# Applying the per-chunk triangular inverses ahead of the recurrence in a one-core RWKV-7 and attention step

## The chip, the core and the metric

The kernel runs on one core of one Trainium2 chip, in float32 throughout. The metric is the device time of one execution in microseconds (us), the median of several runs. The engines are named as in the profile: PE is the matrix engine (TensorE), PEld its weight loads, DVE the vector engine, ACT the scalar engine, POOL GpSimd, and SP the engine whose queue issues most of the DMAs. A name such as L503 is line 503 of the kernel before; where a line of the changed kernel is meant, the text says so.

## What is computed

One inference step of one layer: a combined projection of 1,024 prompt tokens and 32 sample tokens (8 sequences of 4) by `w_in` (1,024 x 9,344), then two branches side by side, RWKV-7 time mixing and dilated window attention, then a gated merge, an output projection and a layer norm. The change lies in the RWKV-7 branch. Its recurrence in the reference, for 8 heads of 64 with the state S[value, key]:

```python
def step(S, inp):
    r_t, w_t, k_t, v_t, kk_t, a_t = inp
    sa = jnp.einsum('bhvk,bhk->bhv', S, -kk_t)
    S = (S * w_t[:, :, None, :] + sa[..., None] * (kk_t * a_t)[:, :, None, :]
         + v_t[..., None] * k_t[:, :, None, :])
    return S, jnp.einsum('bhvk,bhk->bhv', S, r_t)
```

## The kernel before

**Products.** The projection is cut into columns of 128 (`project_steps`, L174). Each has its weights split into a high and a low part (L162 on ACT, L163 on DVE) and takes 72 matmuls of 128 x 352 (`mm3`, L172, tile `pj`); the scheduler below hands them out in pieces of four. These "products" are most of PE's work. Twelve columns (key, receptance, value for four pairs of heads) feed the recurrence, one (columns 1536 to 1663) its decay and its a; 24 others are "fill" (gates, written to DRAM through the tile `zt`) and can run at any time. The very first column is the gate column 1664, done while the input is still being transposed; then comes column 1536, then the stage with streams.

**The recurrence.** A unit is a pair of heads and half of the sequence (512 tokens), so there are 8 units; a unit has 8 chunks of 64 tokens, each with its two heads. For a chunk the token-by-token recurrence becomes matrices: with kappa the normalised key times the running decay, A the 64 x 64 lower triangle of a chunk, and T its inverse. `unit` (L309) prepares a unit: norm of the keys (L313, `rsqrt`), the two small lora products (L294), decay (L330 to L337: `lam`, `E`, `Ei`), kappa and rho in the tile KR (L346, L347), the tile BK (L355, L356), the masked triangles AT (16 matmuls in two halves, L370, masked on DVE in L377), the bonus (L389), the transposed values (L397) and keys (L407), and R0 (L416). `inverse` (L429) inverts the 32 x 32 diagonal blocks on DVE (L441, L444) with the blocks carried through DRAM; `scan` (L454) joins the blocks to the 64 x 64 inverses (L467, L477) and then walks through the 8 chunks one after another:

1. pr = (rho, kappa) times state (L496); R = pr + R0 on DVE (L498).
2. u = inverse times R: two 64 x 64 x 64 matmuls, one a head (L503); ACT negates and copies it into W (L504).
3. new state from W and BT (L508), scaled and added on DVE (L511).

So a chunk has three matmul steps on PE with a DVE or ACT instruction between each two. At the unit's end L519 computes the outputs of all chunks, and `norm` normalises them (L548 transposes).

**The order on PE** is written by `run_streams`, a planner inside the kernel. Four generators (`scans`, `norms`, `inverses`, `units`) yield pairs of numbers: what the step costs PE and how long to wait before the next step. At each turn the first generator whose waiting time is over goes on; if none can, four product matmuls are put in the queue, counted as 0.59 us. The other engines' queues are filled by a scheduler outside of the kernel's text. In `unit`, L331 waits until the scan of the unit two back is done, since the tiles E and KR have two buffers; everything of the preparation from E on stands behind that line.

## Time and profile before

| | us |
|---|---|
| median of 3 runs (lowest, highest) | 1380.13 (1377.95, 1381.62) |
| the profiled execution's own time | 1381.54 |
| its span, first to last instruction | 1379.8 |
| PE busy in the span | 1344.1 |
| first matmul of the first unit (L313) | at 76.78 |
| last matmul of the recurrence's streams (L548) | at 616.88 |

The profiled execution is 1.41 us above the median. Starts of instructions on PE are exact, ends of matmuls are modelled: a matmul of 128 x 352 is shown with 0.3 us though one starts every 0.16 us. So what PE's time goes into is read here from the distances between starts, not from the busy column: a row "x4" is four matmuls in a run, and the next row's start less its own is what it took PE.

### The profile page before, as it was taken

What the parts mean: (1) busy time and instruction counts of PE and PEld (TensorE: products, weight loads), DVE (VectorE), ACT (ScalarE), POOL (GpSimd) and SP (SyncE); (2) the same over time, 40 slices, a digit from 0 to 9 for tenths busy, and PEclk for the clock granted to TensorE, in tenths of its full rate; (3) what the DMA queues carried; (4) which work ended last, traced back from release to release, by engine and by line L of the source; (5) the groups of instructions that cost most, each with busy time, mean ns of one, the idle gap of its engine ahead of it and who ended that gap; (6) DMA issues with size and microseconds to landing.
All of it is one profiled execution on the core that took longest, in us unless ns stands there. A gap on an engine that the chain in (4) does not pass through costs nothing.

```text
span 1379.8 us, 25342 instructions
## 1 busy us (share of the span) xinstructions
PE 1344.1 (97%) x9809; PEld 1245.0 (90%) x9809; DVE 804.0 (58%) x2203; ACT 467.2 (34%) x1089; POOL 67.2 (5%) x82
## 2 busy tenths in 40 slices
PE   7999999999999999999999999999999999899997
PEld 7998998898988889999999999999999998799786
DVE  4358767677867757441555275437542845665565
ACT  4333434444344444431332333233323234132211
POOL 0000000000000000000100000000000000015100
PEclk9999999999999999999999999999999999999999
DMA  6112222412322242336645355635554556795221
GB/s 216 55 47 73 58 82 72 110 37 75 88 59 75 74 110 79 91 94 123 136 106 132 84 141 115 131 93 140 114 123 115 133 122 153 230 287 170 82 103 68
DMA packets 340270, 151.62 MB, mean 110 GB/s; under 512 B 188928, under 2 KB 329622, under 8 KB 339894
## 3 DMA queue, kind: packets, MB, share of 16 engines
q1 hardware_dynamic: 241270, 129.68, 34.6%
q10 hardware_dynamic: 98880, 20.32, 7.4%
q8 instruction: 77, 1.26, 0.4%
q14 instruction: 43, 0.35, 0.1%
HBM read 110.68 MB, written 38.97 MB: 108 GB/s over the span
## 4 chain that ended last, share of the span: by engine, by line
PE 74%; DVE 14%; DMA 7%; issue 2%; ACT 2%; SPq 1%; DVEq 0%; ACTq 0%
PE pj L172 52%; PE pj L1378 7%; DVE tm L441 2%; DVE X L444 2%; PE o L932 2%; DMA cb<-cd 2%; PE s L895 2%; DMA wraw<-in_w_in_dram 1%; DVE wlo L163 1%; DVE o L1178 1%; PE t L915 1%; PE sc L503 1%; PE s L1014 1%; PE g L370 1%; DVE AT L377 1%
## 5 line engine op out<-in xcount | busy, mean ns | idle before, releaser
L172 PE MATMUL pj<-xhi,whi 128*128 128x352 f32 x1848 | 398.7, 337 | 5.0 <-ACT xhi L1245 3.0
L172 PE MATMUL pj<-xlo,whi 128*128 128x352 f32 x1848 | 382.8, 328 | 0.0
L172 PE MATMUL pj<-xhi,wlo 128*128 128x352 f32 x1848 | 381.9, 328 | 0.4 <-DVE wlo L163 0.4
L172 PEld LDWEIGHTS pj<-xhi,whi 128*128 128x128 f32 x1848 | 302.9, 189 | 21.7 <-issue 10.5
L172 PEld LDWEIGHTS pj<-xhi,wlo 128*128 128x128 f32 x1848 | 307.6, 189 | 3.6 <-issue 1.2
L172 PEld LDWEIGHTS pj<-xlo,whi 128*128 128x128 f32 x1848 | 307.9, 189 | 2.5 <-issue 0.4
L163 DVE TENSOR_TENSOR wlo<-wraw,whi 128x512 fp32r<-128x512 f32 x162 | 113.4, 701 | 84.0 <-ACT whi L162 83.3
L162 ACT ACTIVATE whi<-wraw 128x512 fp32r<-128x512 f32 x162 | 100.6, 625 | 146.6 <-PE pj L172 89.0
L905 ACT ACTIVATE Sm<-Sm,nm 128x128 f32<-128x128 f32 (+1 forms) x96 | 42.4, 442 | 102.7 <-DVE nm L902 102.7
L511 DVE SCALAR_TENSOR_TENSOR st<-sc,E,SD 64x64 f32<-64x64 f32 x128 | 36.2, 283 | 47.7 <-PE sc L508 46.2
L441 DVE TENSOR_TENSOR tm<-Y,X 128x60 f32<-128x60 f32 (+24 forms) x248 | 52.6, 212 | 6.3
L444 DVE TENSOR_TENSOR X<-X,tm 128x60 f32<-128x60 f32 (+24 forms) x248 | 52.0, 210 | 6.4
L1378 PE MATMUL pj<-wl,mh 128*128 128x512 f32 (+1 forms) x136 | 52.0, 382 | 0.0
L897 DVE CUSTOM_DVE_ANT_0 Sm<-s,cst 128x128 f32<-128x128 f32 (+1 forms) x96 | 29.2, 346 | 39.0 <-PE s L895 38.3
L494 ACT ACTIVATE SD<-st,E 128x128 f32<-128x128 f32 x64 | 25.6, 400 | 58.5 <-DVE st L511 58.5
L758 POOL TENSOR_TENSOR kvp<-vv,kv 128x512 f32<-128x512 f32 x16 | 19.7, 1233 | 514.3 <-DVE Ss L766 387.0
L932 PE MATMUL o<-PT,Vt 128*128 128x128 f32 x280 | 38.7, 276 | 0.8 <-ACT PT L919 0.8
L895 PE MATMUL s<-k,q 128*128 128x128 f32 (+1 forms) x192 | 37.8, 326 | 1.7 <-DVE ml L897 1.6
L820 ACT ACTIVATE k<-pj 128x352 f32<-128x352 f32 (+1 forms) x36 | 16.2, 454 | 67.5 <-PE pj L172 60.9
L932 PEld LDWEIGHTS o<-PT,Vt 128*128 128x128 f32 x280 | 36.4, 191 | 1.5 <-ACT PT L919 1.1
L503 PEld LDWEIGHTS sc<-R,AT 64*64 64x64 f32 x256 | 19.7, 134 | 18.4 <-DVE R L498 7.9
L299 ACT ACTIVATE zt<-pj,der 128x352 f32<-128x352 f32 x48 | 26.4, 551 | 27.9 <-PE pj L172 26.7
(314 smaller groups left out, 1719.1 us busy)
## 6 DMA issues: line engine op xcount, KB each, us to landing
wraw<-in_w_in_dram SPq DMA_DIRECT2D x146, 256.0 KB
gd<-zt SPq DMA_DIRECT2D x48, 176.0 KB
gt<-gd SPq DMA_DIRECT2D x48, 176.0 KB
vs<-bt ACTq DMA_DIRECT2D x48, 128.0 KB
kc<-in_cache_kv_g_dram SPq DMA_DIRECT2D x48, 128.0 KB
Vt<-vs ACTq DMA_DIRECT2D x12, 512.0 KB
cb<-cd SPq DMA_DIRECT2D x12, 512.0 KB
zd<-zt SPq DMA_DIRECT2D x24, 176.0 KB
```

The source lines that it names most:

```text
L162: S.activation(hi[:], raw[:], AF.Copy)
L163: V.tensor_tensor(lo[:], raw[:], hi.bitcast(F32)[:], ALU.subtract)
L172: T.matmul(out, w[wi][:, n % 4, :], x[:, n % 4, :], start=first and n == 0, stop=last and n == 11)
L441: V.tensor_tensor(tm, Y[:, r : r + 1, r + 1 : 32].to_broadcast([P, m, n]), X[:, 0:m, r : r + 1].to_broadcast([P, m, n]), ALU.mult)
L444: V.tensor_tensor(X[:, 0:m, r + 1 : 32], X[:, 0:m, r + 1 : 32], tm, ALU.subtract)
L503: T.matmul(pu[u, 64 * e : 64 * e + 64], AT[u, e, c, u], R[u, 64 * e : 64 * e + 64], start=True, stop=True)
L511: V.scalar_tensor_tensor(S1[d, d], pS[d, d], E[d, c, 64:65], SD[d, d], ALU.mult, ALU.add)
L895: T.matmul(r, qT[:, i * P : (i + 1) * P], kT[:, keys[i][0] * P : keys[i][0] * P + n], start=True, stop=True)
L897: V.tensor_tensor_reduce(out=Sm[:, i, 0:n], in0=r, in1=m3 if g == 2 else m12[:, 256 - n : 256], scale=1.0, scalar=NEG, op0=ALU.add, op1=AL ...
L905: S.activation(Sm[:, i, 0:n], Sm[:, i, 0:n], AF.Exp, scale=SCALE, bias=nm[:, x : x + 1], accum_out=ml[:, g, 1, i : i + 1])
L932: T.matmul(po[:, (i % 4) * P : (i % 4 + 1) * P], st["Vt"][:, kb_, :], PT[:, n * P : (n + 1) * P], start=m == 0, stop=m == len(keys[i]) - 1,)
L1378: T.matmul(pb[:], a[:, k], wk, start=x == 0, stop=x == len(prods) - 1)
```

## The change

Four things are changed together.

**Inverses applied beforehand.** `scan` transposes kappa once for a unit (4 transposes, and two copies into kT), applies all 16 inverses to kappa in one batch of 16 matmuls (64 x 64 x 64), writes the result over kappa in KR, then applies all 16 inverses to R0 in a second batch of 16. In a chunk, step 2 above is gone: the sum pr + R0 on DVE is written to W directly. A chunk has two matmul steps.

**Preparation before the wait.** In `unit` the wait for the scan two back moves behind Ei, the normalised key, bt, f2, k2 and BK; behind it stay E, KR and rk.

**The planner.** D_HOP goes from 0.99 to 1.25, D_PM from 0.53 to 0.9, D_AT from 7.0 to 3.5, D_WU is gone, D_U0 is new. And `units` and `norms` may only go on while `small`, the planner's sum of small work not yet followed by products, is below 1.0.

**The first projection** is column 1536 (decay and a); column 1664 joins the fill.

The diff, cut to its core:

```diff
     lam = t_()
     V.tensor_tensor_scan(lam[:], rmask, sg[:], 0.0, ALU.mult, ALU.add)
-    while done["scan"] < 2 * j + hf - 1:
-        yield None
-    E = mk(rp, [P, 8, 65], "E", 2)
...
     V.tensor_tensor(BK[:, :, 0:4:3, :], c2p(k2), c2p(Ei), ALU.mult)
+    yield (0.45, 0.0)
+    while done["scan"] < 2 * j + hf - 1:
+        yield None
+    E = mk(rp, [P, 8, 65], "E", 2)
...
+    KR = mk(rp, [P, 4, 4, 64], "KR", 2)
+    V.tensor_tensor(KR[:, :, 1:3, :], c2p(kkn), Ev[:, :, :, 0:64], ALU.mult)
+    V.tensor_tensor(KR[:, :, 0:4:3, :], c2p(Mr[:, sl]), Ev[:, :, :, 1:65], ALU.mult)
     rk = t_()
...
+    pk = ps("sc")
+    for c2 in range(4):
+        T.transpose(pk[:, c2 * P : (c2 + 1) * P], KR[:, c2, 1:3, :], ident)
+    kT = mk(rp, [P, 512], "sz", 2).rearrange("p (a b) -> p a b", a=4)
+    for p in range(2):
...
+        S.activation(kT[u], pk[v, :].rearrange("p (a b) -> p a b", a=4), AF.Copy)
+    yield (0.45, 0.5)
...
+    pk = [ps("sc") for p in range(2)]
+    for c2, p, e in chunks:
+        u = slice(64 * (1 - p), 64 * (1 - p) + 64)
+        T.matmul(
+            pk[p][64 * e : 64 * e + 64, 64 * c2 : 64 * c2 + 64],
+            kT[u, c2, 64 * e : 64 * e + 64], AT[u, e, 2 * c2 + p, u], start=True, stop=True,
+        )
+    for p in range(2):
+        S.activation(KR[:, :, 1 + p, :], pk[p][:, 0:256].rearrange("p (a b) -> p a b", a=4), AF.Copy, scale=-1.0)
+    yield (1.0, D_PM)
+    pu = ps("sc")
+    for c2, p, e in chunks:
+        u = slice(64 * (1 - p), 64 * (1 - p) + 64)
+        T.matmul(
+            pu[u, c2 * P + 64 * e : c2 * P + 64 * e + 64],
+            AT[u, e, 2 * c2 + p, u], R0[u, c2, 64 * e : 64 * e + 64], start=True, stop=True,
+        )
+    S.activation(R0[:], pu.rearrange("p (a b) -> p a b", a=4), AF.Copy, scale=-1.0)
+    yield (1.0, D_U0)
...
-        R = mk(rp, [P, P], "R", 1)
-        V.tensor_tensor(R[u], pr[u, 0:P], R0[u, c2, :], ALU.add)
+        V.tensor_tensor(W[u, c, :], pr[u, 0:P], R0[u, c2, :], ALU.add)
         S.activation(Ot[v, c2, :], pr[v, 0:P], AF.Copy)
         yield (0.2, D_HOP)
-        pu = ps("sc")
-        for e in range(2):
-            T.matmul(pu[u, 64 * e : 64 * e + 64], AT[u, e, c, u], R[u, 64 * e : 64 * e + 64], start=True, stop=True)
-        S.activation(W[u, c, :], pu[u, 0:P], AF.Copy, scale=-1.0)
-        yield 0.4, D_WU
...
-                if x[0] <= now:
+                if x[0] <= now and (small < SMALL or x in own or not prods):
```

The order of PE's instructions in the middle of a unit's scan before, from one chunk's step 1 to the next one's; L172 are products, `st` is the state:

```order
L496 MATMUL sc_3530<-st_115_795,KR_2276 128x128
L172 MATMUL pj_3444<-xhi_8_86,whi_3543 128x352 x4
L172 MATMUL pj_3444<-xhi_8_86,wlo_3544 128x352 x4
L503 MATMUL sc_3555<-R_3532,AT_2350 64x64 x2
L172 MATMUL pj_3444<-xlo_10_88,whi_3543 128x352 x4
L508 MATMUL sc_3572<-W_2443,BT_2459 128x128
L172 MATMUL pj_3445<-xhi_7_85,whi_3449 128x352 x4
```

And the same place in the changed kernel, where products are L173, step 1 is L535 and step 3 is L541:

```order
L535 MATMUL sc_3687<-st_99_692,KR_2201 128x128
L173 MATMUL pj_3547<-xhi_8_86,whi_3693 128x352 x4
L173 MATMUL pj_3547<-xhi_8_86,wlo_3694 128x352 x4
L173 MATMUL pj_3547<-xlo_10_88,whi_3693 128x352 x4
L541 MATMUL sc_3712<-W_2460,BT_2478 128x128
L173 MATMUL pj_3548<-xhi_8_86,whi_3693 128x352 x4
```

The inverse's pair of matmuls is gone; three product rows stand between step 1 and step 3 where two and one stood around it. Before and now three follow step 3.

The order on PE before, at the end of the triangles' first half (L370) and in what follows:

```order
L370 MATMUL g_3917<-KR_3830,BK_3839 128x128
L467 MATMUL sc_3935<-T_743_3928,AT_3131 32x32 x16
L370 MATMUL g_3954<-KR_3830,BK_3839 128x128
...
L477 MATMUL sc_3966<-AT_3131,T_743_3928 32x32 x16
L548 MATMUL g_3985<-ident_69,Ot_3216 128x128 x4
L389 MATMUL g_3997<-t_3842,cst_76 128x512
L496 MATMUL sc_4003<-st_114_794,KR_3043 128x128
```

In the changed kernel, between the triangles' two halves (L378):

```order
L378 MATMUL g_4598<-KR_4534,BK_4337 128x128
L173 MATMUL pj_4549<-xlo_9_87,whi_4553 128x352 x4
L173 MATMUL pj_4550<-xhi_7_85,whi_4553 128x352 x4
L378 MATMUL g_4617<-KR_4534,BK_4337 128x128
L378 MATMUL g_4618<-KR_4534,BK_4337 128x128
```

In six of the eight units the two halves, the transposes and the bonus stood together without a product; at least two product rows now part the halves, and three or more part the second half from the bonus (L397 of the changed kernel).

SP's queue near the start before, from the last load of the input on:

```order
L112 DMA m_233<-in_x_sample_dram 32x1024
L200 DMA zd_89<-zt_274 128x352
L225 DMA m_345<-in_w_w_dram 64x512
L226 DMA m_345<-in_w_a_dram 64x512
L227 DMA cst_76<-in_cst_dram 128x896
L223 DMA so_343<-in_state_rwkv_shift_dram 104x128
L200 DMA zd_89<-zt_304 128x352
L159 DMA wraw_373<-in_w_in_dram 128x4x128
```

The same place in the changed kernel:

```order
L113 DMA m_239<-in_x_sample_dram 32x1024
L260 DMA srow_107<-in_state_rwkv_shift_dram 104x128
L276 DMA cst_76<-in_cst_dram 128x896
L160 DMA wraw_388<-in_w_in_dram 128x4x128
L160 DMA wraw_430<-in_w_in_dram 128x4x128
```

The stores of the first projection's result (`zd<-zt`) no longer stand ahead of the next projection's weights (`wraw`).

122 lines of the change are left out of this document (65 added, 57 removed).

## The prediction

> **What bounds the kernel now.** I read the page first (busy time, chain), then the stage of the recurrence in windows, then its timeline on PE.
>
> ```profile
> PE 1344.1 (97%) x9809; PEld 1245.0 (90%) x9809; DVE 804.0 (58%) x2203; ACT 467.2 (34%) x1089; POOL 67.2 (5%) x82
> PE 74%; DVE 14%; DMA 7%; issue 2%; ACT 2%; SPq 1%; DVEq 0%; ACTq 0%
> ```
>
> PE is the bound: 97% busy, and 74% of the chain. The change touches the stage from the first unit's first matmul to the last unit's transposes. Two windows over it, first all of PE, then the products (L172) alone:
>
> ```profile
> 76.77:616.88 540.11, 529.21 (x4349) 1.00 0.27 76
> 76.77:616.88 540.11, 415.40 (x2234) 1.00 0.27 76
> ```
>
> The stage holds 2234 product matmuls. The pace of products is in the timeline of one chunk on PE (start, duration, instruction):
>
> ```profile
> 350.26 0.44 PE L503 MATMUL sc<-R,AT 64*64 64x64 f32 x4
> 350.63 0.91 PE L172 MATMUL pj<-xhi,wlo 128*128 128x352 f32 x4
> 351.38 0.38 PE L508 MATMUL sc<-W,BT 128*128 128x128 f32 x2
> 351.52 0.89 PE L172 MATMUL pj<-xlo,whi 128*128 128x352 f32 x4
> 352.25 0.81 PE L172 MATMUL pj<-xhi,whi 128*128 128x352 f32 x4
> 352.89 0.81 PE L172 MATMUL pj<-xhi,wlo 128*128 128x352 f32 x4
> 353.54 0.38 PE L496 MATMUL sc<-st,KR 128*128 128x128 f32 x2
> 353.68 0.89 PE L172 MATMUL pj<-xlo,whi 128*128 128x352 f32 x4
> 354.42 0.81 PE L172 MATMUL pj<-xhi,whi 128*128 128x352 f32 x4
> 355.15 0.44 PE L503 MATMUL sc<-R,AT 64*64 64x64 f32 x4
> ```
>
> An undisturbed row of four products takes 0.645 us (352.25 to 353.54 is two), so the stage's products are 2234/4 x 0.645 = 360 us. The other 180 us are small matmuls and waiting. After the stage PE still has products of its own, without streams, until the attention begins, so a shorter chain of chunks buys nothing by itself: what counts is PE's time, the small matmuls and the gaps around them. Whatever is saved there moves all that follows forward. The end of the stage is the one place where something else could hold the time: a chain of DMAs into the attention. There PE waited once:
>
> ```profile
> 658.64 0.91 PE L172 MATMUL pj<-xhi,wlo 128*128 128x352 f32 x4 [0.41 <-DVE wlo L163]
> ```
>
> That chain starts with the store of the last fill product, which moves with the products; I cost it at nothing.
>
> **Term 1, the inverses' matmuls.** In the chunk above L503 costs its own 0.37 us (350.26 to 350.63), 0.09 us in the row ahead of it (354.42 to 355.15 is 0.73), and 0.10 us in the row behind (0.75): 0.56 us. L508 costs 0.14 + 0.08. The lengthened row ahead appears in front of L503 alone, not in front of L508 or L496 (0.64 and 0.65).
>
> Removed are 64 of these. Ten stand next to other small work instead of between products and save only the 0.37 and a little, so 54 x 0.56 + 10 x 0.43 = 34.5 us.
>
> Added in a unit are 4 transposes of 128 x 128 and two batches of 16 matmuls of 64 x 64 x 64. Their nearest rows are L397, four such transposes, and L416, which is exactly one such batch:
>
> ```profile
> 207.74 0.60 PE L397 MATMUL g<-ident,m 128*128 128x128 f32 x4
> 208.09 0.89 PE L172 MATMUL pj<-xhi,whi 128*128 128x352 f32 x4
> 104.64 1.15 PE L416 MATMUL g<-W,AT 64*64 64x64 f32 x32
> 105.72 0.59 PE L172 MATMUL pj<-xhi,wlo 128*128 128x352 f32 x2
> ```
>
> The transposes take 0.35 + 0.08; a batch takes 1.08, with 0.19 for the rows around it 1.27 us. Eight units: 8 x (0.43 + 2 x 1.27) = 23.8 us. The batch is cheap since matmuls in different halves of the array overlap: 32 in 1.08 us, where L503's four, all in one quarter, take 0.37. The bound from above is a batch at L503's pace, 8 x 0.37 = 2.96 us; I take L416, whose batch has the new ones' shape and alternates between halves as they do.
>
> The Trainium skill has a rule against that, in "TensorEngine Tiling (Array Packing)", Restrictions and Gotchas, Gotcha 1 (PSUM Pressure): different row tiles cannot access one PSUM bank at the same time. The second new batch writes one bank from both halves. L416 does just that too and takes 1.08 us, so the row speaks against the rule here; it stays a rival.
>
> Net: 34.5 - 23.8 = 10.7 us less work on PE. DVE's work is the same in kind and count; ACT loses 64 copies and gains five a unit, and is 34% busy: nothing.
>
> **Term 2, PE's waits inside the stage.** The unit that runs beside a scan, on PE:
>
> ```profile
> 201.69 1.16 PE L370 MATMUL g<-KR,BK 64*128 64x128 f32 x16
> 202.78 0.69 PE L467 MATMUL sc<-T,AT 32*32 32x32 f32 x32
> 203.63 1.75 PE L370 MATMUL g<-KR,BK 64*128 64x128 f32 x16 [0.15 <-DVE AT L377]
> 205.31 0.69 PE L477 MATMUL sc<-AT,T 32*32 32x32 f32 x32
> 205.96 0.66 PE L548 MATMUL g<-ident,Ot 128*128 128x128 f32 x4
> 206.56 1.12 PE L389 MATMUL g<-t,cst 128*128 128x512 f32 x2
> 207.52 0.38 PE L496 MATMUL sc<-st,KR 128*128 128x128 f32 x2
> 209.79 0.66 PE L407 MATMUL g<-ident,BK 128*128 128x128 f32 x4 [0.43 <-ACT W L400]
> ...
> 95.90 1.03 PE L389 MATMUL g<-t,cst 128*128 128x512 f32 x2
> 96.36 1.21 PE L172 MATMUL pj<-xhi,whi 128*128 128x352 f32 x4
> 97.41 0.60 PE L397 MATMUL g<-ident,m 128*128 128x128 f32 x4
> ```
>
> The first half of L370 takes 1.09 us, the second 1.68: +0.59, waiting bank by bank for DVE's masks. L467 takes 0.85 against L477's 0.65: +0.20. L548 takes 0.60 against 0.35 for L397: +0.25. L389 takes 0.96 against 0.46 in the unit at 95.90: +0.50. L407 waited 0.43. That is 1.97 us a unit and, over the six units that have this pattern, 11.8. The groups of the whole kernel show what the first two units and the chunks add:
>
> ```profile
> L370 PE MATMUL g<-KR,BK 64*128 64x128 f32 x256 | 22.4, 288 | 3.5 <-DVE AT L377 2.7
> L503 PE MATMUL sc<-R,AT 64*64 64x64 f32 x256 | 28.5, 232 | 2.6 <-DVE R L498 2.3
> L377 DVE TENSOR_TENSOR AT<-g,cst 128x512 f32<-128x512 f32 x32 | 20.7, 683 | 8.8 <-PE g L370 8.8
> L400 ACT ACTIVATE W<-g 64x512 f32<-64x512 f32 x16 | 9.5, 592 | 16.7 <-PE g L397 16.6
> ```
>
> 3.5 us idle in front of L370, nearly all in the first two units, and 2.6 in front of L503; with waits hidden under modelled ends I put the chunks at 4. In all some 19 us.
>
> What stays of them? Two masks take 1.37 us; two product rows between the halves take 1.38, where the wait was about 1 us with 0.85 us or less in between: it goes, and with three or more rows ahead of the bonus so do the 0.25 and the 0.50: 6 x 1.54 = 9.2, and 2.5 of the first two units' 3.5. In a chunk, step 1 to step 3 is now three rows, 2.17 us as from 351.38 to 353.54, for one DVE add and the hops; 3 of the 4 go. L407 keeps its 0.43. Late next: L397, one row behind the bonus in the changed order, where the unit at 95.90 shows a row of 1.05 instead of 0.73: 8 x 0.32 = 2.6 back. And the new batches: copies on ACT, between 0.4 and 1.2 us a link, stand behind each of the transposes, the joins and the first batch, under two rows (1.4 us) each. Bounds: 0 where ACT is free, 0.6 for a split of weights in front of the copy in each of three links, 14 us in all; I take 2, since ACT is mostly idle. Sum: 9.2 + 2.5 + 3 - 2.6 - 2 = 10 us gained, with bounds from 0 (each wait replaced by another) to 17.
>
> **Term 3, the start.** SP's queue and PE:
>
> ```profile
> 25.11 0.33 SPq L200 DMA_DIRECT2D zd<-zt  x1
> 25.49 1.01 SPq L159 DMA_DIRECT2D wraw<-in_w_in_dram  x2
> ...
> 29.46 0.75 PE L172 MATMUL pj<-xhi,whi 128*128 128x352 f32 x3 [1.29 <-ACT whi L162]
> ```
>
> The second projection's weights were issued at 25.49, behind a store that waited for the first projection's result. Now no such store is ahead of them; they are there early, and PE's 1.29 us go. The new first projection needs the parameters transposed sooner; the transposes keep their place on PE, and four banks of `pj` cover DVE and ACT: nothing, 1 us at most if a bank comes free late. The gate column moved to the fill is the same 72 products.
>
> **The rest.** The preparation ahead of the wait adds no instruction. The wait now holds E, KR and rk back; behind it on PE stands only the unit's own L370, and the planner's 3.5 before it is six rows, 3.9 us, for one ACT exponential and three DVE operations of 0.7: covered.
>
> Sum: 1381.54 - 10.7 - 10 - 1.3 = 1359.5 us against the profiled execution, which is 1.41 above the median, so 1358 us.
>
> **Rivals.**
>
> *The waits stay* and only terms 1 and 3 come: 1380.1 - 12 = 1368. For it: DVE is as busy as before in the same stretches. Against: two rows now stand where the masks were waited for. Chance 0.17.
>
> *The new batches wait* for ACT at every link, 14 us instead of 2: 1358 + 12 = 1370. For it: ACT works in order and weight splits stand in its queue. Against: 34% busy. Chance 0.10.
>
> *Slower, by DVE.* The preparation's five operations of 0.68 to 0.74 us that moved ahead of the wait now stand in DVE's queue between the chunks' adds and state updates of a running scan, 3.5 us a unit. If PE waits for all of it in the six units beside a scan, 21 us, and no old wait goes, 1380.1 - 12 + 21 = 1389. It decides from 2 us a unit on. Against: a chunk's hop has 2.17 us for about 0.8 us of work. Chance 0.03.
>
> *The batches don't overlap*: matmuls in different halves go one after another, at L503's pace. The second batch alone: 8 x 1.9 = 15 us, 1373; both: 1388. Against it: L416. Chance 0.02. The rule of the Trainium skill named above ("TensorEngine Tiling (Array Packing)", Gotcha 1) would have it so for the second batch.
>
> **How the numbers follow.** The forecast, 1358, has 0.68: I let it span 1350 (17 us of waits gone) to about 1364. The range 1350 to 1370 takes in the first rival and the milder half of the second. A measurement of this kernel tells 0.3%, 4 us, from no change: faster needs under 1376. That leaves the DVE rival and both batches in series on the other side. Faster 0.94, same 0.03, slower 0.03.
>
> **What would show it.** Term 1: no group of four at 64 x 64 in a chunk, chunk periods of 4.3 us where it was 4.89 for the same six product rows, batches of about 1.1 us. Term 2: L378 of the changed kernel in two halves of 1.1 us each, and little idle in front of step 3 (L541). Term 3: no idle near 28 us. I am wrong if chunks keep 4.9 us, if the batches take near 3 us, or if waits in front of L510, L520 or L541 add up to more than 10 us.

## The result, and the profile after

The changed kernel takes 1372.07 us (median of 4 runs, 1369.35 to 1375.78) against 1380.14 before: a ratio of 0.9945, 95% interval 0.9918 to 0.9972. It is faster by 8 us; 22 were forecast, and the time lies 2 us above the forecast's range. Its profiled execution took 1375.78 us, the slowest of the four.

The page's first part after, and three of PE's groups in the stage (from the first L320 to the last L581): step 1 of a chunk, the triangles, the second batch.

```profile
PE 1334.1 (97%) x10097; PEld 1245.4 (91%) x10097; DVE 794.6 (58%) x2203; ACT 471.4 (34%) x1065; POOL 66.7 (5%) x82
...
L535 PE MATMUL sc<-st,KR 128*128 128x128 f32 x128 | 26.4, 288 | 4.3 <-DVE st L544 3.9 <-ACT whi L163 0.3
...
L378 PE MATMUL g<-KR,BK 64*128 64x128 f32 x256 | 20.9, 295 | 7.6 <-DVE AT L385 3.9 <-DVE KR L363 2.3 <-DVE BK L354 1.3
...
L520 PE MATMUL sc<-R,AT 64*64 64x64 f32 x256 | 9.2, 221 | 0.0
```

Step 1 before:

```profile
L496 PE MATMUL sc<-st,KR 128*128 128x128 f32 x128 | 25.3, 279 | 0.0
```

The new batch waits for nothing. The triangles, in front of which PE idled for 3.5 us before, now have 7.6 us of idle time ahead of them, and step 1, which waited for nothing, has 4.3, nearly all of it for the state's update.

The table of stretches, the stage and what follows it (length; busy time of PE, PEld, DVE, ACT and POOL with the number of instructions in brackets; granted clock of PE; share and GB/s of the DMA engines):

```profile
63.27:614.54 551.27, 535.59 (x4748) 501.55 (x4748) 366.00 (x1268) 229.09 (x490) 5.49 (x20) 0.99 0.28 78
614.54:1374.00 759.46, 741.49 (x4986) 687.74 (x4983) 399.92 (x864) 215.49 (x526) 60.27 (x52) 0.99 0.54 132
```

The stage lasts 551.3 us where it was 540.1, but 2,344 product matmuls lie in it where there were 2,232 (72 of them are the gate column that used to run ahead of it). A product matmul takes 0.162 us, so 112 are 18.1 us, and **the stage at equal products** went from 540.1 to 533.2 us. The stage begins 13.5 us earlier, of which the 72 moved products are 11.6: the start gained 1.9. That makes 8.8 us; the profiled executions differ by 5.8. The missing 3.0 us were lost behind the stage, in code that is the same. There the clock was halved for 3.4 us three times, once in the profile before (both halve it once more at the very end). A second measure used below takes that out: **the time at full clock** is the time less the share of the clock not granted, times the span. Over their runs it is 1373.5 us before and 1362.5 after: 11 us.

Where the work went: rows of the timeline after (start, duration, instruction), first the batches, then a chunk in which nothing is late.

```profile
262.06 0.69 PE L510 MATMUL sc<-AT,sz 64*64 64x64 f32 x32
262.68 0.92 PE L173 MATMUL pj<-xhi,wlo 128*128 128x352 f32 x4
...
264.17 1.15 PE L520 MATMUL sc<-R,AT 64*64 64x64 f32 x32
265.25 0.91 PE L173 MATMUL pj<-xhi,whi 128*128 128x352 f32 x4
...
267.29 0.38 PE L535 MATMUL sc<-st,KR 128*128 128x128 f32 x2
...
269.45 0.38 PE L541 MATMUL sc<-W,BT 128*128 128x128 f32 x2
...
271.58 0.38 PE L535 MATMUL sc<-st,KR 128*128 128x128 f32 x2
```

From start to start, the second batch takes 1.08 us and the first only 0.62; a chunk takes 4.29 us (267.29 to 271.58). Both as forecast or better. With 0.62, 8 x 0.46 = 3.7 us more come from the work than the 10.7 forecast, some 14 us in all (an estimate, since the removed work was not measured apart). The stage at equal products lost only 6.9, so what is lost in it beside the work grew by some 7 us. Part of that is the clock: three windows of half clock of 3.4 us lie in the stage, at 104, 244 and 288, where there was one, at 303. Such a window costs up to 1.7 us, so up to 3.4 of the 7 us are half clock and the rest is waiting.

One late update shows how. First PE, from step 3 of one chunk to step 1 of the next; then DVE in the same 3 us:

```profile
348.25 0.38 PE L541 MATMUL sc<-W,BT 128*128 128x128 f32 x2
...
349.74 0.79 PE L173 MATMUL pj<-xlo,whi 128*128 128x352 f32 x4
351.24 0.46 PE L535 MATMUL sc<-st,KR 128*128 128x128 f32 x2 [0.70 <-DVE st L544]
```

```profile
347.53 0.30 DVE L536 TENSOR_TENSOR W<-sc,R 64x128 f32<-64x128 f32 x1
347.85 0.69 DVE L347 SCALAR_TENSOR_TENSOR t<-t,t 128x512 f32<-128x512 f32 x1
348.46 0.21 DVE L452 TENSOR_TENSOR X<-X,tm 128x60 f32<-128x60 f32 x1
348.59 0.68 DVE L353 SCALAR_TENSOR_TENSOR BK<-t,t 128x512 f32<-128x512 f32 x1
349.19 0.68 DVE L351 TENSOR_TENSOR t<-m,t 128x512 f32<-128x512 f32 x1
349.91 0.28 DVE L544 SCALAR_TENSOR_TENSOR st<-sc,E,SD 64x64 f32<-64x64 f32 x1
350.11 0.68 DVE L354 TENSOR_TENSOR BK<-t,t 128x512 f32<-128x512 f32 x1
350.80 0.29 DVE L544 SCALAR_TENSOR_TENSOR st<-sc,E,SD 64x64 f32<-64x64 f32 x1
```

Step 3 started at 348.25; the update's second half ended at 351.09, 2.84 us later. Three product rows cover 2.17. DVE takes its operations one after another, and in its queue operations of the next unit's preparation (L347 to L354) and of an inverse (L452) stand ahead of the update and even between its two halves. Before, in the chunk that the prediction shows, step 3 (L508) started at 351.38, and both halves of the update were done 1.37 us later:

```profile
352.17 0.58 DVE L511 SCALAR_TENSOR_TENSOR st<-sc,E,SD 64x64 f32<-64x64 f32 x2
```

Such updates can be counted. Step 3 is two matmuls in PE's rows (x2); from the start of the second one to the end of the update (of its first half, where another operation stands between the halves) it takes **over 1.7 us in 15 of 64 chunks, before the change in 3 of 64**. Counted in full, from the start of the first matmul to the end of the second half, more than the 2.17 us that three rows cover are needed in 14 chunks, before the change in none.

The masks are late in the same way:

```profile
362.29 1.16 PE L378 MATMUL g<-KR,BK 64*128 64x128 f32 x16
363.38 0.92 PE L173 MATMUL pj<-xlo,whi 128*128 128x352 f32 x4
364.14 0.80 PE L173 MATMUL pj<-xhi,whi 128*128 128x352 f32 x4
366.23 0.48 PE L378 MATMUL g<-KR,BK 64*128 64x128 f32 x2 [1.28 <-DVE AT L385]
```

```profile
364.81 0.68 DVE L577 TENSOR_TENSOR Ot<-Ot,nt 128x512 f32<-128x512 f32 x1
365.41 0.17 DVE L452 TENSOR_TENSOR X<-X,tm 128x16 f32<-128x16 f32 x1
365.49 0.68 DVE L385 TENSOR_TENSOR AT<-g,cst 128x512 f32<-128x512 f32 x1
```

The first half's matmuls were done by about 363.4 (first fence, PE), but the first mask started on DVE at 365.49 (second fence), behind a chain of operations of a norm and an inverse that ends with the two rows shown. The two product rows were there, as the order had promised; DVE was not.

### The profile page after: what moved, and what is told of

Same layout as the page of the kernel before. It is cut to its first block, busy times and chain, and to the rows that moved or that the text cites. A ratio compares the mean times of both kernels' runs of the same rounds, so it can differ in the third digit from the quotient of the medians.

```text
span 1374.0 us, 25946 instructions
## 1 busy us (share of the span) xinstructions
PE 1334.1 (97%) x10097; PEld 1245.4 (91%) x10097; DVE 794.6 (58%) x2203; ACT 471.4 (34%) x1065; POOL 66.7 (5%) x82
## 3 DMA queue, kind: packets, MB, share of 16 engines
q8 instruction: 79, 1.29, 0.4%
## 4 chain that ended last, share of the span: by engine, by line
PE 79%; DVE 14%; DMA 4%; issue 2%; SPq 1%; ACT 1%; DVEq 0%; ACTq 0%
PE pj L173 57%; PE pj L1421 7%; PE o L975 2%; PE s L938 2%; DVE X L452 2%; DVE tm L449 2%; DMA cb<-cd 1%; PE g L378 1%; PE t L958 1%; PE s L1057 1%; DVE wlo L164 1%; PE sc L535 1%; DVE st L544 1%; DMA cd<-nE 1%; PE sc L541 1%
## 5 line engine op out<-in xcount | busy, mean ns | idle before, releaser
L173 PE MATMUL pj<-xhi,whi 128*128 128x352 f32 x1848 | 400.5, 338 | 4.4 <-ACT xhi L1288 3.1
L173 PE MATMUL pj<-xhi,wlo 128*128 128x352 f32 x1848 | 384.3, 329 | 0.0
L173 PE MATMUL pj<-xlo,whi 128*128 128x352 f32 x1848 | 383.8, 329 | 0.0
L173 PEld LDWEIGHTS pj<-xhi,whi 128*128 128x128 f32 x1848 | 303.9, 190 | 22.2 <-issue 11.9
L173 PEld LDWEIGHTS pj<-xlo,whi 128*128 128x128 f32 x1848 | 310.8, 191 | 2.9 <-issue 2.4
L173 PEld LDWEIGHTS pj<-xhi,wlo 128*128 128x128 f32 x1848 | 309.3, 190 | 2.6 <-issue 1.2
L452 DVE TENSOR_TENSOR X<-X,tm 128x60 f32<-128x60 f32 (+24 forms) x248 | 52.0, 210 | 5.1
L544 DVE SCALAR_TENSOR_TENSOR st<-sc,E,SD 64x64 f32<-64x64 f32 x128 | 36.1, 282 | 29.6 <-PE sc L541 27.4
L533 ACT ACTIVATE SD<-st,E 128x128 f32<-128x128 f32 x64 | 25.6, 401 | 62.8 <-DVE st L544 62.6
L536 DVE TENSOR_TENSOR W<-sc,R 64x128 f32<-64x128 f32 x64 | 18.4, 288 | 31.4 <-PE sc L535 30.3
```

The costliest lines, as they stand in the source:

```text
L173: T.matmul(out, w[wi][:, n % 4, :], x[:, n % 4, :], start=first and n == 0, stop=last and n == 11)
L452: V.tensor_tensor(X[:, 0:m, r + 1 : 32], X[:, 0:m, r + 1 : 32], tm, ALU.subtract)
L544: V.scalar_tensor_tensor(S1[d, d], pS[d, d], E[d, c, 64:65], SD[d, d], ALU.mult, ALU.add)
```

## The experiments

Sixteen kernels, in four groups. "Late" is the count just explained; "stage" is the stage at equal products, of the profiled execution (not meant for kernels whose products ran out). The time at full clock is a median over the runs. The granted clock is known to 0.001, which rounds each value by up to 0.7 us, and the runs of one kernel spread over 2 to 7 us, so a difference of 1 us between two kernels says nothing.

| kernel | median us | ratio to before (95%) | at full clock | stage | late |
|---|---|---|---|---|---|
| before | 1380.1 | | 1373.5 | 540.1 | 3 |
| changed | 1372.1 | 0.9945 (0.9918-0.9972) | 1362.5 | 533.2 | 15 |
| batches only | 1388.0 | 1.0057 (1.0035-1.0079) | 1375.7 | 547.2 | 24 |
| changed, late preparation | 1370.6 | 0.9928 (0.9909-0.9948) | 1362.3 | 531.0 | 18 |
| changed, D_AT 7.0 | 1372.0 | 0.9944 (0.9924-0.9965) | 1366.3 | 534.1 | 13 |
| changed, no limit | 1399.4 | 1.0131 (1.0103-1.0159) | 1377.0 | 551.4 | 17 |
| limit only | 1380.6 | 1.0012 (0.9999-1.0025) | 1373.0 | 541.8 | 2 |
| batches and limit | 1373.9 | 0.9962 (0.9945-0.9979) | 1365.7 | 533.4 | 18 |
| late preparation, D_ST 2.13 | 1375.0 | 0.9967 (0.9957-0.9977) | 1363.3 | 529.9 | 17 |
| late preparation, limit 0.5 | 1366.6 | 0.9916 (0.9899-0.9934) | 1361.7 | 528.4 | 21 |
| late preparation, no inverse on DVE | 1352.0 | 0.9806 (0.9792-0.9819) | 1346.1 | 513.2 | 2 |
| before, no inverse on DVE | 1373.9 | 0.9961 (0.9949-0.9973) | 1368.6 | 534.4 | 1 |
| limit 0.5, D_INV 1.8 | 1418.0 | 1.0276 (1.0261-1.0290) | 1377.2 | | 12 |
| late preparation, inverse on POOL | 1426.1 | 1.0340 (1.0326-1.0354) | 1390.4 | 586.3 | 4 |
| late preparation, low parts on POOL | 1395.9 | 1.0123 (1.0108-1.0137) | 1379.6 | 557.1 | 17 |
| limit 0.5, low parts on POOL | 1390.7 | 1.0080 (1.0063-1.0096) | 1377.3 | 550.2 | 25 |
| limit 0.5, inverse in pieces of two | 1365.0 | 0.9883 (0.9867-0.9900) | 1359.5 | 525.5 | 22 |
| the same, D_INV 0.6 | 1421.0 | 1.0290 (1.0274-1.0307) | 1379.1 | | 13 |

A note on the texts on record: their "stalls" are the stage's length less the sum of its groups' own durations, and count the first batch with 1.08 us instead of the 0.62 that it takes. For the batched kernels the stalls are 3.6 us larger than stated there (28.9 in the changed kernel, 26.0 with late preparation, 42.8 with batches only).

### Which of the four parts

**Batches only**: the kernel before, with the batches, the two-step chunk and their delays.

```diff
 # the kernel before, plus the diff's part in scan() and
-D_PM, D_HOP, D_ST, D_GN, D_IN, D_WU = 0.53, 0.99, 1.54, 12.6, 11.0, 0.48
+D_PM, D_HOP, D_ST, D_GN, D_IN, D_U0 = 0.9, 1.25, 1.54, 12.6, 11.0, 1.2
```

> The kernel before with only the inverses batched: kappa's transposes, the two batches, the two-step chunk and their delays in the planner (D_HOP 1.25, D_PM 0.9, D_U0 1.2); the preparation stays behind the wait, D_AT stays 7.0, no limit on small work, column 1664 first. In the changed kernel's trace the stage's work on PE shrank by the forecast 10 us but its waits grew from 21.9 to 25.3 us. Theory 1 (the moved preparation does it: its DVE operations stand in DVE's in-order queue between a running scan's updates, so PE waits some 10 us ahead of step 1, and the halved D_AT leaves the masks late): batching alone gets the 10 us of work and at least 3 us of the chunks' waits, 1380 - 13 = 1367 us, and shows less than 4 us of waits ahead of step 1. Theory 2 (the shorter chunk itself does it: with one hop fewer, step 1 follows the state's update more closely, whatever DVE is given besides): waits ahead of step 1 stay near 10 us and the time is 1380 - 10 + 5 = 1375 us.

1388.0 us: slower than before, and neither theory had it. The stage at equal products is 7.1 us longer although some 14 us of work are gone: 21 us more are lost, by the batches alone and with the preparation where it always was; up to 7 of them are half clock (17.1 us at half clock in the stage, 3.4 before). Theory 1, that the moved preparation brings the waits, is dead as the main cause. Two other things are seen in the timeline of this kernel, from step 3 of one chunk (L533) to step 1 of the next (L527):

```profile
302.01 0.49 PE L533 MATMUL sc<-W,BT 128*128 128x128 f32 x2
302.34 0.95 PE L313 MATMUL g<-cst,t 128*128 128x2 f32 x8
303.22 0.49 PE L294 MATMUL g<-lorh,lhi 64*128 64x512 f32 x1
305.41 0.79 PE L294 MATMUL g<-lorh,lhi 64*128 64x512 f32 x1 [1.70 <-DVE nt L317]
...
306.99 0.79 PE L527 MATMUL sc<-st,KR 128*128 128x128 f32 x2
```

Small steps of two generators (L533 and L527 of a scan, L313 and L294 of a unit) stand in a row without a product, one of them waits 1.70 us for DVE with nothing to cover it, and the clock is halved from within that wait on (L527's pair takes 0.44 us from its start to the next row's, where step 1 took 0.14).

**Late preparation**: the changed kernel with the wait, E and KR back in their places in the kernel before, D_AT back at 7.0.

```diff
+    while done["scan"] < 2 * j + hf - 1:
+        yield None
+    E = mk(rp, [P, 8, 65], "E", 2)
...
-    yield (0.45, 0.0)
-    while done["scan"] < 2 * j + hf - 1:
-        yield None
-    E = mk(rp, [P, 8, 65], "E", 2)
...
-D_PN, D_KR, D_AT, D_G, D_W, D_INV, D_UP = 0.65, 1.81, 3.5, 0.2, 2.09, 0.9, 14.4
+D_PN, D_KR, D_AT, D_G, D_W, D_INV, D_UP = 0.65, 1.81, 7.0, 0.2, 2.09, 0.9, 14.4
```

> The changed kernel with the preparation back behind the wait and D_AT back at 7.0; batches, first projection and the limit on small work stay. Theory 1 (moved preparation and halved D_AT bring the waits): the 10 us ahead of step 1 shrink to under 4 and units 0 and 1 lose their 3.7 us ahead of the triangles, while the masks of the later units wait as before the change (some 9 us): 1372 - 8 = 1364 us. Theory 2 (the shorter chunk, or the limit): waits as in the changed kernel, 1372 us within 2.

1370.6 us, and the same time at full clock (1362.3 against 1362.5): the move of the preparation and the shorter D_AT together are worth nothing either way, and 18 updates are late where 15 were. Theory 1 falls here too.

**D_AT back at 7.0, nothing else** (the last two lines of the diff above).

> The changed kernel with D_AT alone back at 7.0, the preparation still ahead of the wait. Under theory 1 with D_AT as the larger part: the 11 us that PE waits ahead of the two halves of the triangles fall to 3 or 4, and 1372 - 7 = 1365 us. Under theory 1 with DVE's queue as the larger part: the waits ahead of step 1 stay (10 us), the triangles' go only in units 0 and 1 (3.7 us): 1368 us. If the masks are late because DVE reaches them late whenever they come, no change: 1372 us.

1372.0 us. The waits ahead of the triangles went (L378 waited 1.4 us for its masks, 3.9 in the changed kernel, and none of the first two units' 3.6 is left), and came back ahead of step 1: L535 waited 8.5 us for L544 where it was 3.9. No gain, as in the third variant, though not by its reason. Late preparation differs from this kernel in the move alone. It is 1.4 us faster in the medians, with intervals that overlap, and 4.0 us at full clock (1362.3 against 1366.3): the early preparation has a small cost, which the shorter D_AT made up for.

**No limit on small work.**

```diff
-SMALL = 1.0
+SMALL = 1e9
```

> The changed kernel with the limit on small work taken away (SMALL out of reach), so that units and norms go on whenever their delay is over. If the limit itself brings waits by holding back units and so bunching their steps, 1372 - 5 = 1367 us. If it spreads the small steps as it says, without it more small work stands in a row and more waits: 1375 to 1378 us. Theory 1 sets nothing on it: 1372 within 2, with the waits ahead of step 1 and of the triangles as they are.

1399.4 us, 27 more than with the limit, and 19 more than before the change. No theory had that size. About half of it is left at full clock (1377.0 against 1362.5); the other half is the clock, which fell to 0.984 where the changed kernel has 0.993 (medians of their runs).

### What the limit is worth, and to whom

**The limit alone**, on the kernel before.

```diff
+SMALL = 1.0
...
-                if x[0] <= now:
+                if x[0] <= now and (small < SMALL or x in own or not prods):
...
+                small = max(0.0, small - piece)
```

> The kernel before with only the limit on small work in the planner; nothing batched, preparation, delays and first projection as before. The limit is worth 27 us in the changed kernel (1399 without it, 1372 with). Theory A (small steps of several generators that fall due together stand in a row on PE, whichever they are, and the limit puts products between them): it gains here too, the 9 us that the triangles' masks, transposes and bonus wait in a row, 1380 - 8 = 1372 us. Theory B (only the batches make steps collide, the limit mends what they break): no change, 1380 us within 3. Slower (1385) if units held back leave the scan without inverses in time.

1380.6, no change: theory B. **Batches and limit**, on the kernel before:

> The kernel before with the inverses batched and the limit on small work; preparation, D_AT and first projection as before. Batching alone gave 1388 us. Theory A and B both: the limit takes the waits that batching alone showed (39 us of stalls in the stage against 22) back to some 22, 1388 - 15 = 1373 us, 2 us above the kernel with late preparation (1370.6), which differs from this one in the first projection alone. If first projection and limit hang together some other way, this one is above 1377.

1373.9, as both theories had it. So the parts don't add up one by one: at full clock the limit alone gives 0, the batches alone cost 2, both together give 8, the first projection another 3 (batches and limit against late preparation, which differ in it alone, 1365.7 and 1362.3), the early preparation with the shorter D_AT 0. The limit is not a helper of its own: it takes back waits that the shorter recurrence brings.

**A longer delay behind step 3**, on late preparation:

```diff
-D_PM, D_HOP, D_ST, D_GN, D_IN, D_U0 = 0.9, 1.25, 1.54, 12.6, 11.0, 1.2
+D_PM, D_HOP, D_ST, D_GN, D_IN, D_U0 = 0.9, 1.25, 2.13, 12.6, 11.0, 1.2
```

> The changed kernel with late preparation (D_AT 7.0) and with D_ST at 2.13 instead of 1.54: four product rows instead of three between a chunk's step 3 and the next step 1, 2.8 us instead of 2.17. If step 1 waits because the update of the state reaches DVE behind one other operation (0.7 us), the 10 us of stalls around step 1 shrink to some 3: 1370.6 - 6 = 1365 us, and the mean clock rises to 0.996. If DVE is late by more than one operation at few places, or the recurrence, longer by 64 x 0.6 us, runs out of products, no gain or a loss: 1370 to 1376 us.

1375.0: not the 1365 of the first variant, but in the range of the second. Step 1 did wait less for the update (0.6 us in all, 3.5 before the edit), but updates were as late as before (17), and other waits came up: the norm's L580 waited 3.1 us for masks, and right behind the stage PE waited 5.2 us for ACT (L862) with the clock halved for 6.8 us around it, since the products had been used up in the longer recurrence. The stage at equal products came out no longer (529.9 against 531.0). So the run does not show that more cover behind step 3 is useless; there were not enough products for it.

**A tighter limit**, on late preparation:

```diff
-SMALL = 1.0
+SMALL = 0.5
```

> The changed kernel with late preparation (D_AT 7.0) and the limit at 0.5 instead of 1.0. If small steps in a row are still what costs (19 us of waits are left in the stage beside the clock's windows), a tighter limit gains 3 to 5 us: 1366 us. If the limit at 1.0 already parts them all, 1370.6 within 2; above 1374 if units come so late that the scan waits for its inverses.

1366.6 us, the 4 us expected in the medians; at full clock it is 0.6, and the stage 2.6 shorter. Most of it is that the clock was halved less often.

### The queue of DVE

What stands ahead of the late updates, where the preparation keeps its place, is more than anything else the inverse, 62 short operations a unit: in late preparation it is 16.0 of the 27.2 us that DVE works on other things between step 3 and the end of such an update (the 15 that take over 2.17 us in full). In the changed kernel it is 7.6 of 26.6 us, and the five moved operations of the preparation are 7.2: one stands where the other stood. The inverse's operations were left out, in the batched kernel and, as the control, in the one before:

```diff
-            tm = mk(rp, [P, 80], "tm", 2)[:, 0 : m * n].rearrange("p (a b) -> p a b", a=m)
-            V.tensor_tensor(
-                tm, Y[:, r : r + 1, r + 1 : 32].to_broadcast([P, m, n]), X[:, 0:m, r : r + 1].to_broadcast([P, m, n]), ALU.mult
-            )
-            V.tensor_tensor(X[:, 0:m, r + 1 : 32], X[:, 0:m, r + 1 : 32], tm, ALU.subtract)
```

> The kernel with late preparation (limit 1.0, D_AT 7.0), with the 62 DVE operations of each unit's inversion left out: the blocks are carried through DRAM as before, but come back as the identity. PE's order is unchanged. In the batched kernels the state's update ends over 1.7 us after step 3 has started in 15 to 24 of 64 chunks, before the change in 3, and mostly inverse operations stand ahead of it in DVE's queue. Theory C (the two-step chunk waits for DVE behind this queue): those late updates fall from 18 to 5 or fewer, the 10 us of stalls in chunks with three product rows after each step to 4, and the time from 1370.6 to 1363 us. Rival (three rows are too short for the hop itself, whatever DVE has to do): 1369 to 1371 us, stalls around the chunks as they are.

> The control: the kernel before with the same 62 DVE operations of each unit left out. Theory C says that the three-step chunk is seldom late on the update (3 of 64 over 1.7 us): only its step 2, with two rows after step 1, waited for DVE (4 us), so the time falls by 4 us at most, 1379.6 to 1376. Rival (fewer DVE operations help any kernel of this kind): it falls by as much as the batched one does, 7 us or more, to 1372.

The batched kernel fell from 1370.6 to 1352.0 us, by 18.6; the one before from 1379.8 to 1373.9, by 5.9. Late updates are 2 and 1 of 64. PE's waits in the stage of the batched kernel (first) and of the control (second), with the time waited, how often, and the longest:

```profile
PE g L377 <- ACT Ot L577: 1.4, 3, 0.5
PE sc L488 <- ACT T L484: 0.5, 2, 0.4
```

```profile
PE g L407 <- ACT W L400: 2.6, 6, 0.4
PE g L370 <- DVE AT L377: 1.7, 7, 0.4
PE sc L503 <- ACT W L499: 1.0, 2, 0.6
```

In the batched one the view shows no wait for DVE any more. It shows idle time over 0.15 us alone, so it misses much. PE's order is the same with and without the inverse (but for two neighbours in the batched kernel), so the distances between starts on PE can be held against each other one by one. In the batched kernel they sum up to 17.8 us less in the stage: 6.9 in front of step 1, 2.3 each in front of the triangles and of the joins, 1.6 each in front of step 3 and of the lora products, and 3.0 in the product rows. Half clock is in these sums: two windows in the stage with the inverse, none without. In the control they sum up to 5.7 us less, 3.4 of it in front of step 2.

So theory C's mechanism holds: the same operations, taken out, are worth three times as much to the two-step chunk, which waited at step 1, as to the three-step chunk, which waited at step 2. (The two kernels also differ in the limit and the first projection; the limit alone changed nothing in the kernel before.) Its sizes do not hold. It had 7.6 us for the batched kernel and at most 4 for the control, whose 5.9 (interval 3.7 to 7.0) also lies short of the 7 that the rival asked for.

Without the inverse the two kernels differ by **22 us (1352.0 against 1373.9)**, and by 8 to 9.5 us with it. That 22 is also the sum that was forecast for the change is luck. Of the 21.2 us by which the stage differs here, 4.1 are waits in the view (6.0 against 1.9) and up to 1.7 one window of half clock; some 15 are left, mostly the work, where the forecast had 10.7 of work and 10 of waits.

**The inverse handed out half as densely**, with the limit at 0.5:

```diff
-D_PN, D_KR, D_AT, D_G, D_W, D_INV, D_UP = 0.65, 1.81, 7.0, 0.2, 2.09, 0.9, 14.4
+D_PN, D_KR, D_AT, D_G, D_W, D_INV, D_UP = 0.65, 1.81, 7.0, 0.2, 2.09, 1.8, 14.4
```

> Late preparation, limit 0.5 (1366.6 us), and D_INV at 1.8 instead of 0.9: the inverse's operations come half as densely in DVE's queue, over some 30 us a unit instead of 15. Theory C: fewer stand ahead of an update (21 of 64 over 1.7 us fall to 12), 1366.6 - 3 = 1363.5 us. If the inverses now come late for the scan, or the lateness comes from weight splits and masks instead: 1366 to 1370 us.

1418.0 us. Late updates fell to 12 as theory C said, but the recurrence grew longer than its cover: the products ran out ahead of the last scan. The table of stretches at that place, and two steps there:

```profile
622.00:680.00 58.00, 27.77 (x218) 21.22 (x219) 20.74 (x64) 13.06 (x33) 0.00 (x0) 0.50 0.12 31
```

```profile
642.36 0.77 PE L534 MATMUL sc<-st,KR 128*128 128x128 f32 x2 [0.77 <-DVE st L543]
643.50 0.79 PE L540 MATMUL sc<-W,BT 128*128 128x128 f32 x2 [0.37 <-DVE W L535]
645.22 0.77 PE L534 MATMUL sc<-st,KR 128*128 128x128 f32 x2 [0.93 <-DVE st L543]
```

58 us at half clock with 218 matmuls in them. A chunk without products takes 2.86 us at that clock, hops and nothing else. The run tells nothing on theory C's price.

### All the work kept, less of it on DVE

**The inverse on POOL**, late preparation:

```diff
-            V.tensor_tensor(
+            G.tensor_tensor(
...
-            V.tensor_tensor(X[:, 0:m, r + 1 : 32], X[:, 0:m, r + 1 : 32], tm, ALU.subtract)
+            G.tensor_tensor(X[:, 0:m, r + 1 : 32], X[:, 0:m, r + 1 : 32], tm, ALU.subtract)
```

> The kernel with late preparation (limit 1.0, D_AT 7.0, 1370.6 us), with the 62 operations of each unit's inversion on POOL instead of DVE; nothing is left out, PE's order is the same, and POOL is 5% busy. Without these operations the same kernel took 1352.0 us. Theory C (step 1 and the masks wait for DVE behind the inverse's operations): nearly all of that comes, 1354 to 1358 us, and the stage's stalls fall from 22 to below 9 us. POOL's own rows of this size (128x128 in 0.40 to 0.52 us) put the 62 operations at some 25 us a unit instead of 13 on DVE, of a unit's 69: on time unless the scan waits for them. Rivals: the inverses come late for the scan and PE waits ahead of the joins, 1365 us or more; or DVE's operations grow longer beside POOL's and the gain is eaten, 1362 to 1370 us.

1426.1 us, far off. Late updates did fall to 4, but PE waited 13.4 us in one place, 6.0 to 6.4 us in three and 2.3 to 3.1 us in six. What is behind the longest, on SP's queue:

```profile
105.97 0.38 SPq L160 DMA_DIRECT2D wraw<-in_w_in_dram  x1
120.53 0.67 SPq L455 DMA_DIRECT2D Xd<-X  x1
121.31 0.54 SPq L201 DMA_DIRECT2D zd<-zt  x1
```

The store of the inverse (`Xd`) is issued by SP and waits there for POOL, 14.5 us; the stores of `zt` stand behind it, DVE's next `zt` waits for their buffer (15.65 us), the masks stand behind that, and PE waits 13.4 us for a mask. In two other places DVE stood 10 and 11 us at the load of an inverse that was not there yet. The slower inverse (310 to 336 ns an operation instead of 212) was late for what was queued behind it.

**The low parts of the weights on POOL** while the recurrence runs, on late preparation and on the limit at 0.5:

```diff
-        V.tensor_tensor(lo[:], raw[:], hi.bitcast(F32)[:], ALU.subtract)
+        lo_engine[0].tensor_tensor(lo[:], raw[:], hi.bitcast(F32)[:], ALU.subtract)
...
-        G.memset(E[:, :, 0:1], 1.0)
+        V.memset(E[:, :, 0:1], 1.0)
...
+        lo_engine[0] = G
         run_streams()
+        lo_engine[0] = V
```

> The kernel with late preparation (limit 1.0, D_AT 7.0, 1370.6 us), with the low parts of the weights computed on POOL instead of DVE while the recurrence runs (65 operations of 0.69 us on DVE), and E's first column set by DVE instead of POOL. Nothing is left out; PE's order is the same. If what stands in DVE's queue delays updates and masks, whatever it is, freeing 45 of DVE's some 350 us in the stage takes a third of the stalls, which were 18 us by the inverse's 105 us: 1370.6 - 6 = 1365 us. If the inversion itself is what delays them, no change: 1370.6 within 2. If the splits come late from POOL (1.2 us each by its rows of 128x512), the products wait for weights: 1375 us or more.

> The same edit on the kernel with late preparation and the limit at 0.5 (1366.6 us). By the theory of DVE's queue 1366.6 - 5 = 1361.5 us, the fastest of all kernels that leave nothing out; if the inversion itself delays, 1366.6 within 2; if the splits come late from POOL, 1371 us or more.

1395.9 and 1390.7 us: both slower by 24 to 25 us. PE waited for no split; DVE's own operations had grown longer. Three places in the timeline of the first of the two, DVE, POOL and PE:

```profile
163.16 0.18 DVE L450 TENSOR_TENSOR tm<-Y,X 128x24 f32<-128x24 f32 x1
163.37 1.28 DVE L453 TENSOR_TENSOR X<-X,tm 128x24 f32<-128x24 f32 x1
164.69 0.17 DVE L450 TENSOR_TENSOR tm<-Y,X 128x16 f32<-128x16 f32 x1
```

```profile
163.32 1.30 POOL L166 TENSOR_TENSOR wlo<-wraw,whi 128x512 fp32r<-128x512 f32 x1 [9.68 <-ACT whi L165]
```

```profile
165.66 0.49 PE L542 MATMUL sc<-W,BT 128*128 128x128 f32 x2 [0.86 <-DVE W L537]
```

An operation of 0.18 us on DVE, begun beside POOL's, takes 1.28 and ends with it at 164.6; the add of the chunk stands behind it, and step 3 waits 0.86 us. 18 of the inverse's 496 operations took over 1 us in this way, where none did before. So 45 us of work went from DVE and nearly all of it came back: over the stage DVE is busy for 371 us where it was 370, and updates are as late as before. The runs leave open what was to be asked here, since the move brought a delay of its own.

**The inverse handed out in pieces of two operations instead of four**, with the limit at 0.5, once as densely and once thinner (D_INV 0.6):

```diff
-            if r % 2:
-                yield (0.0, D_INV)
+            yield (0.0, D_INV)
...
-D_PN, D_KR, D_AT, D_G, D_W, D_INV, D_UP = 0.65, 1.81, 7.0, 0.2, 2.09, 0.9, 14.4
+D_PN, D_KR, D_AT, D_G, D_W, D_INV, D_UP = 0.65, 1.81, 7.0, 0.2, 2.09, 0.45, 14.4
```

> Late preparation, limit 0.5 (1366.6 us), and the inverse hands out one of its 31 rounds at a time (two DVE operations, D_INV 0.45) instead of two (four operations, D_INV 0.9): as dense, in smaller pieces. If an update is late since it stands behind a group of four (0.85 us on average, up to 1.5), late updates fall from 21 of 64 over 1.7 us to 12 or fewer and the time to 1363.5 us. If DVE's work as a whole is what delays, no change: 1366.6 within 2.

> The same with D_INV 0.6, a third thinner: the inverse is handed out over 18.6 us of the planner's time instead of 14. If density counts, better than the run with 0.45 by 1 to 3 us (1361 to 1363); if the recurrence, longer by some 2 to 4 us a unit, costs more than it brings, 1366 to 1372 us. With D_INV 1.8 for two rounds the products ran out before the last scans and the time was 1418 us; 1.2 for two rounds is a third of that step.

With 0.45 the time is 1365.0 us, the fastest of all kernels that leave nothing out, but late updates stayed at 22, so the size of the pieces is not what makes them late, and against the 1366.6 of the limit at 0.5 the intervals touch. With 0.6 the products ran out ahead of the last scan once more: 1421.0. That cliff is near: in the kernel with 0.45, 2,422 product matmuls lie in the stage, and in the three kernels that went further (D_INV 1.8 and 0.6, D_ST 2.13) 2,468, all that were left for it.

## Why the prediction was wrong, step by step

**Term 1, the work on PE: right, better than forecast.** 10.7 us were forecast, some 14 came, by the estimate above. The second batch and the chunk are as worked out (1.08 and 4.29 us); the first batch takes 0.62 where the row of R0 had promised 1.08. The rival's price for batches that don't overlap (2.96 us each, at L503's pace) is out, and so is the rival of batches that wait for ACT: in front of L510 and L520 PE waited for nothing. The reason given is not shown, though. At the pace of the products, 352 columns in 0.161 us, the 32 matmuls of 64 columns that a batch's row shows would take 0.94 us one after another (an estimate). So 1.08 us, for R0 as for the second batch, does not tell whether the two halves overlap when they write one bank, and L416 does not settle that rival as the prediction has it; the first batch's 0.62 us is faster than that. And no run shows that L503's pace, 0.37 us for four, would hold for 32.

**Term 2, the waits inside the stage: this is the step that failed.** Forecast were 10 us less; measured were some 7 more, of which up to 3.4 are two more windows of half clock. The prediction said of the masks that two product rows cover their 1.37 us and the wait "goes", and of the chunk that 2.17 us of rows stand against "one DVE add and the hops". Both sums hold the duration of DVE's operation against the rows, as if DVE took it up at once. DVE takes its operations one after another, and the runs show that what stands ahead of the one that counts is the larger part: 15 updates of 64 were late where there had been 3, the mask shown started 2 us after its matmuls, and with 62 short operations a unit taken out of the queue the batched kernel loses its waits for DVE and 18.6 us (1352.0), the kernel before only 5.9. The waits were not replaced one by one, as the lower bound of this term had it; they grew.

**The cover of D_AT** was a part of that step ("one ACT exponential and three DVE operations: covered"). It holds for units behind a scan. Units 0 and 1 have no scan to wait for, all of their preparation stands ahead of the triangles, and PE waited 1.3 and 2.3 us there.

**Term 3, the start: right.** 1.3 forecast, 1.9 measured.

**What had no term at all: the limit on small work.** The prediction gave the new rule of the planner neither a gain nor a cost. It decides the sign: without it the changed kernel takes 1399.4 us, 1.3% more than before, and the batches alone 1388.0. Without it PE waits longer for DVE in several places (4.2 us in front of step 3 where it was 0.4, 7.1 in front of step 1 where it was 3.9), though hardly more updates are late (17); the size of the effect was not traced further. The rival on the slower side had the right engine, DVE's queue, and in the main the wrong operations: where the move is the only difference, at D_AT 7.0, it costs 1.4 us in the medians and 4.0 at full clock, not 21, although it is seen in the way in single chunks: there it stands where operations of the inverse stand without the move.

**The signs of being wrong were chosen badly too.** The prediction named waits in front of L510, L520 and L541; there they stayed under 1 us. They came in front of L535, which it did not name, and of L378, which it named only for its length.

What stays open: why the same operations of DVE delay the two-step chunk so much more than the three-step one. It was only argued that the scans got shorter while DVE's work did not: summed over the units, from the start of a unit's first step 1 to that of its last step 3, they last 272 us instead of 313, and DVE is busy for 70% of it instead of 67% (50% without the inverse, in late preparation). That is a small difference, and in the kernel with the limit at 0.5 it is 65%, and 21 updates are late. Nor was it shown which order of DVE's queue would do; no run set that order.

## What to carry to other kernels

A wait of the busiest engine is covered when the helper can *begin* in time, so hold against the cover what stands in the helper's queue at that place, not the duration of the one operation; shortening the chain on the busy engine leaves the helper as much to do in less time. Where a change brings several parts, give each a term, a planner's rule too: here one line decides between 8 us faster and 19 us slower. An operation moved to another engine takes along all that is queued behind its result, DMA issues above all.

## What the runs showed of the hardware

**Half clock after short waits.** PE's clock is halved for 3.413 us or a multiple of it in the traces here (the last window of an execution apart), and one window of 3.413 us costs up to 1.7 us. After the changed kernel's wait for masks at 242:

```profile
242.20 0.48 PE L378 MATMUL g<-KR,BK 64*128 64x128 f32 x2 [1.06 <-DVE AT L385]
242.88 1.16 PE L378 MATMUL g<-KR,BK 64*128 64x128 f32 x14 [0.20 <-DVE AT L385]
243.97 1.50 PE L173 MATMUL pj<-xhi,whi 128*128 128x352 f32 x4
```

A row of four products takes 1.29 us from 243.97 on, twice its 0.65. The waits before it were 1.06 and 0.20 us; waits of 1.28 and 0.19 us in the same two places of another unit, at 366, had no such window, so the length of the waits alone does not decide it. The Trainium skill ("TensorE: Matmul & The Clock Gate", HAM oscillation) gives as the rule that PE should have no idle gap over some 3.4 us. The trace disagrees here: in this place half clock followed waits of little more than a third of that in sum. So a wait can cost PE its length and 1.7 us more. Over the runs the clock not granted, with the window at the very end, is 6.6 us of the kernel before, 9.6 of the changed one and 22.4 of that without the limit.

**POOL's large operations slow DVE down.** A DVE operation on two tiles in SBUF that began while POOL did a 128x512 subtraction (1.29 us) ended with it: 1.28 us for 0.18 in the rows above. The chunk's own operations, which read a tile of PSUM, were not longer beside POOL (0.28 us for the update either way). Beside POOL's short operations of the inverse (0.3 us alone) most of DVE's operations kept their time, but some large ones and POOL's own grew together: around 105 us in that kernel, DVE's of 128x512 take up to 0.80 us instead of 0.69, and POOL's 0.62 to 0.66. The Trainium skill ("GPSIMD Engine Reference", Key points) says that POOL shares its SBUF interfaces with DVE and that DVE instructions with two SBUF inputs meet contention; the trace agrees.

**Sixteen 64 x 64 x 64 products in 0.62 or 1.08 us.** The first batch's go to all four quarters of the array and to two banks, the second's, like R0's, to two quarters and one bank. Four matmuls in one quarter (L503) take 0.37 us. No run told the quarters from the banks.
